# Probability scaling on two engines, half-width projections and a finer gate chain in a diffusion trunk

## The chip, the cores and the metric

The kernel runs on one core of a Trainium2 chip. The metric is the device time of one execution in microseconds (us), median of several runs. A core has five engines that work side by side: TensorE (PE in the profile, its weight loads PEld), VectorE (DVE), ScalarE (ACT), GpSimd (POOL) and SyncE (SP, which here issues DMAs). TensorE writes its results to PSUM, eight banks of 512 f32 columns on 128 partitions.

## The reference, cut to what matters

Two layers of a diffusion trunk over 256 latent and 256 context tokens of width 1024. Each layer is a half-step SwiGLU FFN, a token mixer and another half-step FFN, all with modulated norms. The mixer reads one normalised input `h` and makes three branches from one projection:

```python
qa, ka, va, qb, kb, vb, qm, km, vm, om, gm, gl = split_columns(h @ w_in)
y_a = windowed_attention(rope(qa), ...)                 # branch A, softmax with a sink
y_b = dense_attention(rope(rms_norm(qb)), ...)          # branch B, softmax
y_m = mlstm_mixer((qm, km, vm, om, gm), ...)            # branch C, gates from gm
y = merge(y_a, y_b, y_m, gl, w_branch, w_out)
```

Both attentions have 8 query heads of 64; latent blocks see up to 512 keys, context blocks 256. The mLSTM needs log-sigmoid forget gates, their running sums and a running maximum over each sequence. In the second layer the context tokens have keys and values only, no queries and no output.

## The kernel before, in words

All work is matrix products in split precision. An f32 weight unit of 512 KB (a `raw` tile, 128x1024) is loaded by DMA and turned into a rounded part `hi` by ACT (line 163) and a rest `lo` by DVE (line 164); activations are split likewise (lines 189 and 190). `mm3` (lines 192 to 196) makes one product of three matmuls, hi by hi, hi by lo and lo by hi, summed in PSUM.

The program is a list of tasks, each with the weight units it needs and a function; `run_tasks` issues them in order with loads three units and conversions two units ahead. A scheduler behind it fixes each engine's order of instructions when the program is built, from priorities that follow the program's order; the engines then run in that order and wait on semaphores. Tiles come from pools: eight PSUM banks (`psum`), 13 large SBUF tiles (`slot`), and so on. A new tile of a full pool waits until an old one was last read.

A mixer (`mixer_tasks`, line 830) does the projections `qa`, `qb`, `kk`, `vvg` and `vm` with tasks from `tok_tasks` (line 695): tokens are the stationary operand, 128 at a time, weights the moving one. `qb` and `vm` have 512 columns in four tasks of two k-blocks each (512 KB a task). The first task opens one PSUM bank for each token block (four, or two for `qb` in layer 1), each task adds 6 matmuls of 512 columns to each block, and the last one empties each bank as it finishes: `vm` with a copy on ACT or DVE in turn, `qb` (`q_rows`, line 749) with two ACT reads of the bank, a reduction and, for latent blocks, a rotation on DVE.

Attention (`attn_steps`, line 989) runs in steps, branch A first (x = 0), then branch B (x = 1); 32 steps in layer 0 and 16 in layer 1. A step takes two heads of one block of 128 queries: two score products into two banks, a maximum of each on DVE (line 1016), an exponential of each with its sum on ACT (line 1030), a reciprocal on DVE (line 1039), and the scaling of the two probability tiles E by 1/sum, both on GpSimd (line 1042). Two steps later the tiles are transposed on TensorE (line 1054) into one or two banks and split by ACT and DVE (189, 190), and one step after that multiplied with V (lines 1069 and 1071) into a bank that two steps share.

Other tasks are woven between the steps, to give TensorE work: in branch A the rest of `qb`, `vm`, the mLSTM gates (`mgate_steps`, line 1100) and merge gates computed ahead; in branch B the convolutions. The gates are three tasks: `logsig`, `rows` (16 pairs of small matmuls, then on DVE two copies, five scans and 11 small operations that build the decay rows KR), and `cols`. In layer 0 the first of the four `qb` tasks stands ahead of attention (QC = 1), in layer 1 all of `qb` and the first `vm` task.

Of the kernel before, what the change touches and what calls it, by code (L numbers as in the profile page):

```python
# [10 lines left out]
F32 = mybir.dt.float32  # L11
# [53 lines left out]
class Builder:  # L65
# [41 lines left out]
    def unit_src(self, key):  # L107
# [16 lines left out]
        if kind == "tok":  # L124
            _, l, name, ks, n = key
            src = a["w_" + name][l, ks[0] * P:(ks[-1] + 1) * P, :]
            return src.rearrange("(k p) c -> p k c", p=P), (len(ks), n), True
        if kind == "fm":
# [592 lines left out]

    def by_stream(self, tasks, pre):
# [26 lines left out]
    def q_rows(self, q, src, tb, branch, ss):  # L749
# [9 lines left out]
        sq = self.t512()  # L759
# [3 lines left out]
        if tb < 2:  # L763
            u = self.t512()
            self.rope(u, q, 8, tb, self.cosg[0], self.sing[0], q)
        else:
            self.times_g(q, q, 8, 0)
# [62 lines left out]
    def mixer_tasks(self, l, need_ctx, ms, pre, done, turn):  # L830
# [21 lines left out]
        def qq(x):  # L852
            def f(tb, ps):
                if f"qr{x}" not in R:
                    R[f"qr{x}"] = self.slot([P, 4, T])
                    if x:
                        R["qss"] = self.lp.tile([P, 4, 8], F32, tag="qss", name=self.nm("qss"))
                self.q_rows(R[f"qr{x}"][:, tb, :], ps, tb, x, R["qss"][:, tb, :] if x else None)
            return f
# [25 lines left out]
        def vm(tb, ps):  # L885
# [3 lines left out]
            self.copy(R["vm"][:, tb, :, 0:128], ps.rearrange("p (h d) -> p h d", h=4))  # L889
# [12 lines left out]
        qa = self.tok_tasks(l, "qa", 512, 2, qtb, ms, qq(0))  # L902
        qb = self.tok_tasks(l, "qb", 512, 2, qtb, ms, qq(1))
# [6 lines left out]
        vm_ = self.tok_tasks(l, "vm", 512, 2, range(4), ms, vm)  # L910
# [9 lines left out]
        side = gates[:1] + qb[:1] + gates[1:2] + qb[1:] + vm_[nv:va] + gates[2:] + vm_[va:vb] + qcols(1) + vm_[vb:]  # L920
# [68 lines left out]
    def attn_steps(self, qtb, R):  # L989
# [5 lines left out]
        def score(i):  # L995
# [44 lines left out]
            for e in range(2):  # L1040
                t = E[i][e]
                nc.gpsimd.tensor_scalar(out=t[:, :nkey], in0=t[:, :nkey], scalar1=r[:, e:e + 1], scalar2=None,  # L1042
                                        op0=ALU.mult)
# [56 lines left out]
    def mgate_steps(self, R):  # L1100
# [27 lines left out]
        def rows(_):  # L1128
# [9 lines left out]
            b_r, m_r = RW[:, 2, :], RW[:, 3, :]  # L1138
            i_r, f_r = RW[:, 0, :], RW[:, 1, :]
# [4 lines left out]
            v.tensor_tensor_scan(out=m_r, data0=f_r, data1=i_r, initial=0.0, op0=ALU.add, op1=ALU.max)  # L1144
            KR = self.slot([8, 14, P])
# [33 lines left out]
        return [([], logsig), ([], rows), ([], cols)]  # L1179
# [245 lines left out]
def _layout(inp):  # L1425
# [21 lines left out]
    a["w_qb"] = c(w[:, :, C_QB + qcols])  # L1447
# [47 lines left out]
```

## Time and profile before

| | us |
|---|---|
| median of 3 runs (lowest, highest) | 2273.91 (2273.75, 2274.84) |
| the profiled execution | 2271.84 |
| its span, first to last instruction | 2270.1 |

| engine | busy us | share of the span |
|---|---|---|
| PE | 2195.6 | 97% |
| DVE | 1545.9 | 68% |
| ACT | 984.6 | 43% |
| POOL | 133.0 | 6% |

A row of a timeline gives the start in us from the span's start, the length in us, the engine, the line of the kernel, the instruction, output and inputs by name, shape and how many were merged into the row; in brackets the engine's idle time before it and who ended it. A busy PE counts a matmul until its result has left the array, so matmuls overlap, and the time that one costs is the distance from its start to the next start. Granted clock 1.00 is TensorE's level of 2.4 GHz, 0.50 that of 1.2 GHz.

### The profile page before, as it was taken

How to read it: one execution, taken by the hardware profiler on the slowest of the kernel's cores; microseconds unless marked ns; L12 is line 12 of the kernel's file. 1: busy time of each engine (PE TensorE's matmuls, PEld its weight loads, DVE VectorE, ACT ScalarE, POOL GpSimd, SP SyncE). 2: the span in 40 equal slices, each digit the busy share in tenths (PEclk: the TensorE clock that was granted, in tenths of full speed). 3: DMA queues.
4: the chain of work that ended last, by engine and by line, in shares of the span. 5: the costliest groups of instructions: out<-in, count | busy, mean ns of one | idle time of the engine just before them, and what ended most of it. 6: DMA issues, size and time to landing. Idle time of an engine off the chain costs nothing.

```text
span 2270.1 us, 30607 instructions
## 1 busy us (share of the span) xinstructions
PE 2195.6 (97%) x11666; PEld 1837.6 (81%) x11666; DVE 1545.9 (68%) x2756; ACT 984.6 (43%) x1569; POOL 133.0 (6%) x100
## 2 busy tenths in 40 slices
PE   6999999998999999999999999999999989998998
PEld 4877777787777888888878788777778878997997
DVE  3987775877678664654444378778849787786556
ACT  3322223554588533542222253222226488655444
POOL 0000000013241000000000000000000142000000
PEclk9999999999999999999999999999999999998999
DMA  7665564422213333434433336665634123565554
GB/s 282 214 196 186 165 199 149 125 81 76 94 38 82 119 119 136 142 115 135 129 114 127 103 107 204 195 195 178 223 116 159 57 89 96 167 228 172 189 186 153
DMA packets 126402, 331.36 MB, mean 146 GB/s; under 512 B 12712, under 2 KB 26088, under 8 KB 125488
## 3 DMA queue, kind: packets, MB, share of 16 engines
q1 hardware_dynamic: 111664, 314.02, 43.0%
q10 hardware_dynamic: 14592, 15.40, 2.2%
q8 instruction: 91, 1.49, 0.3%
q14 instruction: 55, 0.45, 0.1%
HBM read 320.91 MB, written 8.47 MB: 145 GB/s over the span
## 4 chain that ended last, share of the span: by engine, by line
PE 84%; DVE 8%; ACT 3%; DMA 2%; issue 2%; POOL 0%; ACTq 0%; POOLq 0%; SPq 0%; DVEq 0%
PE ps L194 26%; PE ps L195 26%; PE ps L196 26%; PE ps L1243 1%; DVE lo L164 1%; DVE sm L1016 1%; ACT t L1030 1%; PE ps L1212 1%; ACT hi L163 1%; PE ps L366 1%; PE ps L1054 1%; PE ps L468 1%; DVE t L190 0%; DVE slot L959 0%; DMA raw<-in_w_gu_dram 0%
## 5 line engine op out<-in xcount | busy, mean ns | idle before, releaser
L163 ACT ACTIVATE hi<-raw 128x1024 fp32r<-128x1024 f32 (+1 forms) x444 | 457.0, 1032 | 766.8 <-PE ps L195 274.7
L194 PE MATMUL ps<-slot,hi 128*128 128x512 f32 (+1 forms) x2232 | 780.5, 351 | 7.7 <-ACT slot L189 5.3
L195 PE MATMUL ps<-slot,hi 128*128 128x512 f32 (+1 forms) x2232 | 776.9, 349 | 0.9 <-DVE slot L190 0.7
L196 PE MATMUL ps<-slot,lo 128*128 128x512 f32 (+1 forms) x2232 | 776.6, 348 | 0.0
L164 DVE TENSOR_TENSOR lo<-raw,hi 128x1024 fp32r<-128x1024 f32 (+1 forms) x444 | 527.1, 1190 | 245.2 <-ACT hi L163 240.7
L194 PEld LDWEIGHTS ps<-slot,hi 128*128 128x128 f32 x2232 | 421.2, 190 | 77.5 <-ACT slot L189 6.6
L195 PEld LDWEIGHTS ps<-slot,hi 128*128 128x128 f32 x2232 | 422.5, 189 | 57.4 <-DVE slot L190 1.7
L196 PEld LDWEIGHTS ps<-slot,lo 128*128 128x128 f32 x2232 | 421.9, 189 | 57.9
L194 PE MATMUL ps<-hi,slot 128*128 128x512 f32 (+2 forms) x1048 | 400.6, 382 | 1.8 <-ACT slot L189 1.1
L196 PE MATMUL ps<-hi,slot 128*128 128x512 f32 (+2 forms) x1048 | 399.5, 382 | 0.0
L195 PE MATMUL ps<-lo,slot 128*128 128x512 f32 (+2 forms) x1048 | 399.5, 381 | 0.0
L358 DVE SCALAR_TENSOR_TENSOR t<-raw,sc,t 128x1024 f32<-128x1024 f32 x224 | 280.5, 1281 | 128.8 <-DMA raw<-in_w_ada_dram 128.5
L1042 POOL TENSOR_SCALAR t<-t,sm 128x512 f32<-128x512 f32 (+1 forms) x96 | 132.9, 1396 | 1767.1 <-DVE sm L1039 1675.7
L194 PEld LDWEIGHTS ps<-hi,slot 128*128 128x128 f32 x1048 | 197.5, 188 | 46.2 <-issue 5.7
L196 PEld LDWEIGHTS ps<-hi,slot 128*128 128x128 f32 x1048 | 197.0, 188 | 39.3
L195 PEld LDWEIGHTS ps<-lo,slot 128*128 128x128 f32 x1048 | 197.3, 188 | 38.8 <-issue 0.2
L189 ACT ACTIVATE slot<-t 128x512 fp32r<-128x512 f32 (+1 forms) x138 | 80.7, 594 | 185.4 <-DVE t L606 160.2
L606 DVE TENSOR_TENSOR t<-ps,t 128x512 f32<-128x512 f32 (+1 forms) x88 | 54.7, 622 | 89.1 <-PE ps L196 87.8
L190 DVE TENSOR_TENSOR slot<-t,slot 128x512 fp32r<-128x512 f32 (+1 forms) x138 | 87.6, 644 | 4.4 <-ACT slot L189 4.1
L1016 DVE TENSOR_REDUCE sm<-ps 128x1 f32<-128x512 f32 (+1 forms) x96 | 54.4, 593 | 22.2 <-PE ps L1015 21.5
L1054 PE MATMUL ps<-ident,t 128*128 128x128 f32 x320 | 47.7, 282 | 18.6 <-POOL t L1042 8.4
L1054 PEld LDWEIGHTS ps<-ident,t 128*128 128x128 f32 x320 | 37.5, 143 | 28.5 <-POOL t L1042 17.3
(198 smaller groups left out, 1670.6 us busy)
## 6 DMA issues: line engine op xcount, KB each, us to landing
raw<-in_w_gu_dram SPq DMA_DIRECT2D x176, 512.0 KB
raw<-in_w_ada_dram SPq DMA_DIRECT2D x128, 512.0 KB
raw<-in_w_down_dram SPq DMA_DIRECT2D x92, 512.0 KB
raw<-in_w_fm_dram SPq DMA_DIRECT2D x64, 512.0 KB
raw<-in_w_br_dram SPq DMA_DIRECT2D x24, 512.0 KB
raw<-in_w_out_dram SPq DMA_DIRECT2D x24, 512.0 KB
slot<-in_w_ada_dram SPq DMA_DIRECT2D x16, 512.0 KB
raw<-in_w_down_dram SPq DMA_DIRECT2D x20, 256.0 KB
```

What stands on the lines that cost most here:

```text
L163: self.nc.scalar.activation(out=hi, in_=raw, func=AF.Copy)
L164: self.nc.vector.tensor_tensor(out=lo, in0=raw, in1=hi.bitcast(F32), op=ALU.subtract)
L189: self.nc.scalar.activation(out=hi, in_=src, func=AF.Copy)
L190: self.nc.vector.tensor_tensor(out=lo, in0=src, in1=hi.bitcast(F32), op=ALU.subtract)
L194: mm(out, lh, rh, start=start, stop=False, **kw)
L195: mm(out, lh, rl, start=False, stop=False, **kw)
L196: mm(out, ll, rh, start=False, stop=stop, **kw)
L358: v.scalar_tensor_tensor(out=acc, in0=units[0], scalar=c, in1=acc, op0=ALU.mult, op1=ALU.add)
L606: nc.vector.tensor_tensor(out=hid[:, :W], in0=ps[:, :W], in1=hid[:, :W], op=ALU.mult)
L1016: v.tensor_reduce(out=mx[:, e:e + 1], in_=ps[:, :nkey], axis=AX.X, op=ALU.max)
L1042: nc.gpsimd.tensor_scalar(out=t[:, :nkey], in0=t[:, :nkey], scalar1=r[:, e:e + 1], scalar2=None, op0=ALU.mult)
L1054: nc.tensor.transpose(pt[:, n * P:(n + 1) * P], e[n % 2][:, kb * P:(kb + 1) * P], self.ident)
```

## The change

Three things are changed.

1. In the attention step GpSimd scales only the first of the two tiles. The second goes to ACT in branch A and to DVE in branch B.
2. `qb` and `vm` are taken in two halves of 256 columns, each half in two tasks of four k-blocks (still 512 KB a task, now contiguous). Two token blocks share one PSUM bank, so that a half holds two banks (one for `qb` in layer 1) where the whole held four (two). A block's half is emptied as it finishes in the second task. The evacuations `q_rows` (branch B) and `vm` work on 256 columns, twice as often.
3. The gate task `rows` becomes three tasks: `rows` (matmuls and copies), `scans` and `decays`. In layer 0 the first four gate tasks are woven with the three `qb` tasks that are left.

```diff
+        if kind == "half":
+            _, l, name, h, g = key
+            return a["w_" + name][l, h, g], (4, 256), True
...
+    def half_tasks(self, l, name, tbs, ms, evac):
+        ds = {}
+        def mk(h, g):
+            def fn(units):
+                u = units[0]
+                for tb in tbs:
+                    if g == 0 and tb % 2 == 0:
+                        ds[h, tb // 2] = self.psum().rearrange("p (b c) -> p b c", b=2)
+                    ps = ds[h, tb // 2][:, tb % 2, :]
+                    for x in range(4):
+                        lh, ll = ms["hi"][g][:, x, tb * P:(tb + 1) * P], ms["lo"][g][:, x, tb * P:(tb + 1) * P]
+                        self.mm3(ps, lh, ll, u[0][:, x, :], u[1][:, x, :], g == x == tb % 2 == 0, g == 1 and x == 3,
+                                 skip_group_check=True)
+                    if g:
+                        evac(tb, h, ps)
+            return ([("half", l, name, h, g)], fn)
+        return [mk(h, g) for h in range(2) for g in range(2)]
...
-        sq = self.t512()
+        sq = self.t512()[:, :256]
...
-            u = self.t512()
-            self.rope(u, q, 8, tb, self.cosg[0], self.sing[0], q)
+            u = self.t512()[:, :256]
+            self.rope(u, q, 4, tb, self.cosg[0], self.sing[0], q)
         else:
-            self.times_g(q, q, 8, 0)
+            self.times_g(q, q, 4, 0)
...
-            self.copy(R["vm"][:, tb, :, 0:128], ps.rearrange("p (h d) -> p h d", h=4))
+            self.copy(R["vm"][:, tb, 2 * h:2 * h + 2, 0:128], ps.rearrange("p (h d) -> p h d", h=2))
...
-        qb = self.tok_tasks(l, "qb", 512, 2, qtb, ms, qq(1))
+        qb = self.half_tasks(l, "qb", qtb, ms, qqb)
...
-        vm_ = self.tok_tasks(l, "vm", 512, 2, range(4), ms, vm)
+        vm_ = self.half_tasks(l, "vm", range(4), ms, vm)
...
-        side = gates[:1] + qb[:1] + gates[1:2] + qb[1:] + vm_[nv:va] + gates[2:] + vm_[va:vb] + qcols(1) + vm_[vb:]
+        side = weave(gates[:4], qb) + vm_[nv:va] + gates[4:] + vm_[va:vb] + qcols(1) + vm_[vb:]
...
             for e in range(2):
-                t = E[i][e]
-                nc.gpsimd.tensor_scalar(out=t[:, :nkey], in0=t[:, :nkey], scalar1=r[:, e:e + 1], scalar2=None,
-                                        op0=ALU.mult)
+                t = E[i][e][:, :nkey]
+                if e and x == 0:
+                    nc.scalar.activation(out=t, in_=t, func=AF.Copy, scale=r[:, e:e + 1])
+                else:
+                    (v if e else nc.gpsimd).tensor_scalar(out=t, in0=t, scalar1=r[:, e:e + 1], scalar2=None, op0=ALU.mult)
...
-        return [([], logsig), ([], rows), ([], cols)]
+        return [([], logsig), ([], rows), ([], scans), ([], decays), ([], cols)]
```

The weights of `qb` and `vm` are laid out by halves on the host, outside the measured time.

## Rows read from the trace of the kernel before

**Rows 1.** The page's head: the span of the profiled execution.
```profile
span 2270.1 us, 30607 instructions
```

**Rows 2.** Busy time by stretch: attention A and B of layer 0, between, layer 1.
```profile
480.00:604.00 124.00, 118.11 (x641) 96.76 (x640) 90.69 (x240) 64.33 (x145) 38.98 (x30) 1.00 0.21 70
604.00:705.00 101.00, 90.58 (x499) 75.81 (x498) 72.17 (x152) 75.86 (x139) 42.81 (x35) 0.98 0.27 79
705.00:1780.00 1075.00, 1072.04 (x5135) 880.90 (x5134) 695.32 (x1169) 400.36 (x591) 0.00 (x0) 1.00 0.44 141
1780.00:1848.00 68.00, 61.06 (x391) 51.29 (x389) 54.83 (x137) 37.32 (x82) 25.32 (x16) 0.97 0.18 60
1848.00:1903.00 55.00, 48.36 (x314) 42.39 (x313) 42.90 (x88) 46.22 (x78) 25.74 (x16) 0.97 0.22 73
```
Columns: stretch, its length, busy us (instructions) of PE, PEld, DVE, ACT and POOL, granted clock, DMA share, GB/s.

**Rows 3.** PE's waits, 480 to 604 us: total us, times, longest.
```profile
PE ps L1054 <- DVE t L190: 3.2, 1, 3.2
PE ps L1069 <- ACT t L1030: 2.0, 1, 2.0
```

**Rows 4.** PE's waits, 604 to 705 us.
```profile
PE ps L1054 <- POOL t L1042: 6.0, 8, 1.2
```

**Rows 5.** PE's waits, 1780 to 1848 us.
```profile
PE ps L1069 <- DVE t L190: 2.2, 2, 1.7
```

**Rows 6.** PE's waits, 1848 to 1903 us.
```profile
PE ps L1054 <- POOL t L1042: 2.4, 3, 1.2
```

**Rows 7.** Groups of instructions by shape on POOL: busy us, mean ns, idle before.
```profile
L1042 POOL TENSOR_SCALAR t<-t,sm 128x512 f32<-128x512 f32 x64 | 102.7, 1616 | 1698.9 <-DVE sm L1039 1648.0 <-ACT t L189 18.1 <-ACT sm L1036 13.3
```

**Rows 8.** Timeline at 647 to 651 us: one step's scalings, then its transposes.
```profile
647.61 3.10 POOL L1042 TENSOR_SCALAR t<-t,sm 128x512 f32<-128x512 f32 x2 [3.75 <-DVE sm L1039]
...
650.77 0.98 PE L1054 MATMUL ps<-ident,t 128*128 128x128 f32 x7 [1.21 <-POOL t L1042]
```

**Rows 9.** Timeline of DVE: start of `rows`' chain, and the split behind it.
```profile
511.83 0.67 DVE L1137 COPY slot<-ps 8x512 f32<-8x512 f32 x1
...
520.22 0.67 DVE L190 TENSOR_TENSOR t<-ps,t 128x512 fp32r<-128x512 f32 x1
```

**Rows 10.** Timeline of PE: matmuls of 512 columns, then of 256.
```profile
522.22 0.40 PE L195 MATMUL ps<-slot,hi 128*128 128x512 f32 x1
...
527.30 0.40 PE L196 MATMUL ps<-slot,lo 128*128 128x512 f32 x1
...
455.06 0.28 PE L195 MATMUL ps<-lo,slot 128*128 128x256 f32 x1
...
458.90 0.28 PE L195 MATMUL ps<-lo,slot 128*128 128x256 f32 x1
```

**Rows 11.** Groups by shape on DVE and ACT, for prices.
```profile
L356 DVE TENSOR_SCALAR t<-raw,sc 128x1024 f32<-128x1024 f32 x32 | 23.5, 750 | 14.5 <-DMA raw<-in_w_ada_dram 14.3 <-DMA t<-in_norm_g_dram 0.2
...
L164 DVE TENSOR_TENSOR lo<-raw,hi 128x1024 fp32r<-128x1024 f32 x416 | 507.8, 1223 | 227.6 <-ACT hi L163 223.1 <-PE ps L196 1.4
...
L164 DVE TENSOR_TENSOR lo<-raw,hi 128x512 fp32r<-128x512 f32 x20 | 13.8, 689 | 16.4 <-ACT hi L163 16.4
...
L453 ACT ACTIVATE t<-slot,sm 128x1024 f32<-128x1024 f32 x10 | 11.5, 1145 | 11.4 <-DVE sm L220 11.4
```

**Rows 12.** Timeline of DVE and POOL where both work at once.
```profile
1872.36 0.62 DVE L1024 TENSOR_TENSOR sm<-sm,qsc 128x2 f32<-128x2 f32 x1
...
1870.74 3.10 POOL L1042 TENSOR_SCALAR t<-t,sm 128x512 f32<-128x512 f32 x2 [5.76 <-DVE sm L1039]
...
1896.17 1.21 DVE L164 TENSOR_TENSOR lo<-raw,hi 128x1024 fp32r<-128x1024 f32 x1
...
1896.35 4.00 POOL L1042 TENSOR_SCALAR t<-t,sm 128x512 f32<-128x512 f32 x2 [5.80 <-DVE sm L1039]
```

**Rows 13.** Groups by shape on ACT: prenorm's second reader of a bank.
```profile
L478 ACT ACTIVATE t<-ps,modT,Amod 128x256 f32<-128x256 f32 x54 | 27.8, 562 | 30.0 <-DVE t L476 22.0 <-PE ps L468 8.0
```

**Rows 14.** Busy time by stretch: one at the lower clock.
```profile
622.10:625.40 3.30, 3.30 (x14) 2.92 (x12) 1.48 (x4) 2.82 (x7) 0.00 (x0) 0.50 0.00 1
```

More of the change, by code (lines that the diff above doesn't have):

```diff
@@ L850, in vv, with qqa, qqb @@
             self.copy(R["gm"][:, tb, :], ps[:, 256:272])
[L852 to L859, printed above, removed]
+        def qqa(tb, ps):
+            if "qr0" not in R:
+                R["qr0"] = self.slot([P, 4, T])
+            self.q_rows(R["qr0"][:, tb, :], ps, tb, 0, None)
+        def qqb(tb, h, ps):
+            if "qr1" not in R:
+                R["qr1"] = self.slot([P, 4, T])
+                R["qss"] = self.lp.tile([P, 4, 8], F32, tag="qss", name=self.nm("qss"))
+            self.q_rows(R["qr1"][:, tb, 256 * h:256 * h + 256], ps, tb, 1, R["qss"][:, tb, 4 * h:4 * h + 4])
         def qcols(x):
@@ L883, in unspill, with vm @@
                 nc.sync.dma_start(self.X[s], self.spill[s])
-        def vm(tb, ps):
+        def vm(tb, h, ps):
             if "vm" not in R:
@@ L901, in mixer_tasks @@
         vt = self.tok_tasks(l, "vvg", 272, 2, range(4), ms, vv)
-        qa = self.tok_tasks(l, "qa", 512, 2, qtb, ms, qq(0))
-        qb = self.tok_tasks(l, "qb", 512, 2, qtb, ms, qq(1))
+        qa = self.tok_tasks(l, "qa", 512, 2, qtb, ms, qqa)
+        qb = self.half_tasks(l, "qb", qtb, ms, qqb)
         conv = [self.conv_task(l, c, ms, R, need_ctx) for c in range(8)]
@@ L1137, in rows, with scans @@
                 v.tensor_copy(RW[:, q, :], ps[:8, :])
-            b_r, m_r = RW[:, 2, :], RW[:, 3, :]
-            i_r, f_r = RW[:, 0, :], RW[:, 1, :]
+            R["RW"] = RW
+        def scans(_):
+            RW = R["RW"]
+            i_r, f_r, b_r, m_r = (RW[:, q, :] for q in range(4))
             for b in range(4):
@@ L1144, in rows, with decays @@
             v.tensor_tensor_scan(out=m_r, data0=f_r, data1=i_r, initial=0.0, op0=ALU.add, op1=ALU.max)
+        def decays(_):
+            RW = R.pop("RW")
+            i_r, f_r, b_r, m_r = (RW[:, q, :] for q in range(4))
             KR = self.slot([8, 14, P])
@@ L1446, in _layout @@
     a["w_qa"] = c(w[:, :, C_QA + qcols])
-    a["w_qb"] = c(w[:, :, C_QB + qcols])
+    halves = lambda m: c(m.reshape(2, 2, 4, P, 2, 256).transpose(0, 4, 1, 3, 2, 5))
+    a["w_qb"] = halves(w[:, :, C_QB + qcols])
     a["w_kk"] = c(np.concatenate([w[:, :, C_KA:C_KA + 128], w[:, :, C_KB:C_KB + 128]], axis=2))
@@ L1450, in _layout @@
     a["w_vvg"] = c(np.concatenate([w[:, :, C_VA:C_VA + 128], w[:, :, C_VB:C_VB + 128], w[:, :, C_GM + gcols]], axis=2))
-    a["w_vm"] = c(w[:, :, C_VM:C_VM + 512])
+    a["w_vm"] = halves(w[:, :, C_VM:C_VM + 512])
     a["w_om"] = c(w[:, :, C_OM:C_OM + 512])
```

## The prediction

> **What bounds the kernel now.** I read busy time by stretch first, then PE's waits in the stretches that fall short. Outside the mixers' attention TensorE is the bound: between the two attentions it is busy 1072.04 of 1075 us [rows 2], so nothing done to other engines there can show. The four attention stretches are where the change acts. PE is idle there for 124.0 - 118.1 = 5.9 us in branch A and 101.0 - 90.6 = 10.4 us in branch B of layer 0, and for 6.9 and 6.6 us in layer 1 [rows 2]. That is 29.8 us, and it is nearly all that the change can win. On top stand short stretches at the lower clock: in one of 3.3 us the granted clock is 0.50 [rows 14], and the means of 0.98, 0.97 and 0.97 in three of the stretches [rows 2] say there is about one in each.
>
> Who ends the idle time differs by branch. In layer 0, branch A, two waits make 5.2 of the 5.9 us: one of 3.2 us for a bank that the split on DVE frees late, one of 2.0 us for a bank that an exponential frees late [rows 3]. In branch B, GpSimd's scaling ends 6.0 of the 10.4 us, in 8 waits [rows 4]. In layer 1, branch A waits mostly for splits on DVE (2.2 us in the largest group, [rows 5]), and branch B for GpSimd (2.4 us, [rows 6]) and for DVE. DVE is busy 90.7 of 124, 72.2 of 101, 54.8 of 68 and 42.9 of 55 us, ACT 75.9 of 101 and 46.2 of 55 us in the two B stretches [rows 2]. So PE is ahead, but DVE and ACT have no more than a fifth to a quarter to spare, and every step is a chain through all of them.
>
> **Scaling on two engines.** Today the two tiles of a step are scaled one after the other, 1.6 us each [rows 7], so the second is ready 3.1 us after the reciprocal. The timeline shows which of the two hurts: after the pair of 3.10 us one transpose has gone ahead and the other seven wait 1.21 us for the second [rows 8]. With the second tile on DVE or ACT the pair is ready when GpSimd's one is, 1.6 us earlier or a little less. In branch B I count half of the 6.0 + 2.4 us as won: the waits for the second tile go, those for the first stay. That is -4.2 us; the ends are 0 (something else comes last) and -8.4.
>
> The work does not vanish. A two-input operation costs 1223 ns at 1024 columns and 689 at 512 [rows 11], so 2 x 689 - 1223 = 155 ns are fixed. The one-input scaling on DVE takes 750 ns at 1024 [rows 11]; with the same fixed part it is 0.45 us at 512 columns and 0.30 at 256. Branch B gives DVE 8 x 0.45 + 8 x 0.30 = 6.0 us in layer 0 and 8 x 0.45 = 3.6 us in layer 1. The trace has no 512-column scaling from SBUF; the ends are half of 750 ns and all of it. DVE rises from 71 to 77% of layer 0's B stretch and from 78 to 85% of layer 1's. Maxima and splits queue behind it, and PE waits for those already. I charge a quarter of the 9.6 us, +2.4 us; the ends are 0 and all of it. ACT's scaled copy is 1145 ns at 1024 [rows 11], by the same split 0.65 us at 512 and 0.40 at 256: 8.4 us in layer 0's A stretch, where ACT is busy 64.3 of 124 us, and 5.2 us in layer 1's, 37.3 of 68 [rows 2]. Exponentials, splits and conversions queue behind it. With half of ACT free I charge nothing; without that cover it would be a quarter of 13.6 us, +3.4.
>
> GpSimd and DVE meet more often now. The trace has both orders. A DVE operation with two SBUF inputs that is already running holds GpSimd up: behind the 1.21 us conversion at 1896.17 the pair that starts at 1896.35 takes 4.00 us where 3.10 is usual. In the other order a tiny DVE operation, 0.08 us behind the start of the pair's second scaling (1870.74 + 1.54), takes 0.62 us for two columns [rows 12]: it ends 0.7 us into GpSimd's 1.56 us, so it waits for the first part of that instruction, not for all of it. DVE's scaling comes right behind the reciprocal on its own engine, while GpSimd has to be told by a semaphore, so I expect DVE first and GpSimd up to 0.45 us later. That is why half of the waits stay in the sum above.
>
> The Trainium skill, "SBUF — State Buffer", section "Who interferes with whom", says that whoever of DVE in a two-port mode and GpSimd issues first holds the shared pair for the whole instruction and the other fully blocks. The first order agrees, the second only in part (0.62 us of 1.56). Taken at its word in the bad order, it is the third rival.
>
> **Halves and shared banks.** `qb` and `vm` have 14 products of one token block (4 + 4 in layer 0, 2 + 4 in layer 1), each 24 matmuls of 512 columns: 336, which become 672 of 256. From 522.22 to 527.30 lie 22 matmuls of 512, 231 ns each; from 455.06 to 458.90 lie 33 of 256, 116 ns each [rows 10]. Two halves cost 1 to 2 ns more than the whole: 336 x 2 = +0.7 us, with PE the bound there. The doubled weight loads stay hidden, as they are in these rows. Loads and conversions keep their number and size. Evacuations double in count, at 155 ns fixed each: a few us on DVE and ACT over both layers, hidden where PE is busy; I charge nothing.
>
> What it gives is room. Through most of branch A four of eight banks are held by an open `qb` or `vm`; two score banks, one for transposes and one for output are all that is left to attention, and the two large waits of [rows 3] are waits for banks. With two held, both should go or shrink. For the first there is a second reason: the chain of `rows` keeps DVE from 511.83 on, and the split that PE waits for stands behind it at 520.22, 8.4 us later [rows 9]. Cut in three, it lets attention's maxima and splits in between; that moves 8 us of DVE work, it removes none, and the last gate task comes one or two side tasks later, with its reader far behind. I take -4.0 of the 5.2 us in layer 0 (ends 0 and -5.2). In layer 1 all of `qb` is before attention, only `vm` holds banks, and the waits are for DVE, which keeps its work: I take -2.0 (ends +2, as five gate tasks now fill steps that have no other product, and -4).
>
> What it costs is a new wait. The second block of a bank may write only when the first has been read out. The trace shows that a bank is passed on as a whole: prenorm reads two separate halves of one bank on DVE and then on ACT, and ACT sat idle 22.0 us before its half until DVE was done, in 7 waits [rows 13], though no data go between them. There are 14 blocks, so 7 such bank pairs per half and 14 handovers. PE can do the other bank's block meanwhile, 12 x 116 ns = 1.4 us, or attention, which stands in the same queue. A reader that is not delayed needs less than that. I charge 0.1 us each, +1.5 us; the ends are 0 and the first rival.
>
> **Sum.** -4.2 + 2.4 + 0.7 - 4.0 - 2.0 + 1.5 = -5.6 us. Of three stretches at the lower clock, each standing behind long waits, I let one go: 3.4 us at half speed is 1.7 us of work, taken as -1.2. Together -6.8 us, against the profiled execution of 2271.84 (span 2270.1, [rows 1], and 1.7 around it): 2265.0. The median of the runs is 2.1 us above that execution, so I forecast **2267 us**.
>
> **Rivals.** *No change,* **2273**. Every step runs through DVE, ACT and PE, and the order on each is fixed beforehand. A wait of 1 us for GpSimd that goes shows the next one, for a maximum or a split, right behind; won and lost waits balance, and only the 0.7 us of columns and the odd wait remain. For it: in branch B no engine is idle more than 30%, and besides GpSimd four other producers end PE's waits. Against: the 3.2 and 2.0 us waits of [rows 3] have a clear cause that the change removes. Chance 0.27. That the change doesn't do what it says is the same case: a scaling ordered so late on DVE that the pair is ready no earlier.
>
> *The bank handover, slower.* If the reader of the first block stands behind a conversion (1.22 us, [rows 11]) before its reads (0.56 us each for 256 columns, [rows 13], two for `qb`, one for `vm`), PE is held 1.22 + 1.12 - 1.4 = 0.9 us at a `qb` handover and about 0.4 at a `vm` one even with the other bank's block as cover, and 2.3 and 1.8 without. With 6 and 8 handovers, all uncovered: 14 + 14 = 28 us; with half of them, 14 us, against the sum without its 1.5, -8.3: 2273.9 + 14 - 8.3 = **2280**. It decides from where readers begin over 1 us after the block's last matmul. The Trainium skill speaks for the wait itself: "PSUM — Partial Sum Buffer", section "PSUM bank collisions raise a hardware error", wants PSUM guarded by bank, not by address; the 22.0 us of [rows 13] agree. Chance 0.10.
>
> *The shared port, slower.* If GpSimd comes first and DVE's scaling waits for its whole 1.56 us (0.8 at 256 columns, by halving), branch B adds 8 x 2.0 + 8 x 1.1 = 25 us of DVE time in layer 0, where 28.8 are free, and 16 us in layer 1, where 12.1 are [rows 2]: layer 1 overruns by 4 us, and a third of layer 0's 25 shows, 8 us; with the -6 of branch A, 2273.9 + 12 - 6 = **2280**. It decides from where DVE has other work between the reciprocal and the scaling. Chance 0.08.
>
> **How the numbers follow.** Forecast 0.55, no change 0.27, the slower two 0.18. About 0.2%, 4.5 us, is what a measurement of this kernel can tell from no change: faster means below 2269.4, slower above 2278.5. The far ends of the gains (-5.2, -4, -8.4 and three clock stretches of 1.7) give 2251; I put the low end at 2255, since all at once is unlikely, and the high end just over the slower rivals, 2281, leaving some 0.05 below and 0.13 above. The forecast's own range is 2255 to 2269.
>
> **What would show it.** Right: the wait of 3.2 us for a split near 521 and that of 2.0 us for an exponential are gone; PE's waits for GpSimd in branch B fall from 8.4 to about 4 us; PE's idle time falls from 29.8 to about 23; DVE's new scaling takes 0.45 us and starts ahead of GpSimd's. Wrong: PE's waits before the second block of `qb` or `vm` for ACT's or DVE's evacuation (handover); scalings of 1 us and more on DVE (port); waits for maxima and splits that grow by what those for GpSimd lose (no change).

## The result, and the profile after

The changed kernel is slower: a median of 2286.39 us (2284.68 to 2291.26) against 2273.83 us (2273.63 to 2274.84) for the kernel before on the same chip, a ratio of 1.0060 (95% interval 1.0048 to 1.0072). That is 12.6 us, and outside the predicted range. The profiled execution took 2286.34 us, its span is 2284.6 us: 14.5 us more than before's.

Busy time by stretch in the changed kernel, with the same columns as [rows 2] and bounds at the same work (attention A and B of layer 0, between, attention A and B of layer 1):

```profile
480.00:609.00 129.00, 116.91 (x782) 103.75 (x781) 92.88 (x260) 74.92 (x171) 19.16 (x15) 0.97 0.22 71
609.00:715.00 106.00, 92.47 (x522) 77.56 (x522) 76.65 (x165) 74.86 (x139) 21.63 (x17) 0.98 0.24 70
715.00:1791.00 1076.00, 1073.65 (x5201) 883.96 (x5200) 698.46 (x1186) 401.54 (x595) 0.00 (x0) 1.00 0.44 142
1791.00:1859.00 68.00, 61.52 (x454) 55.75 (x453) 53.38 (x132) 41.72 (x91) 12.51 (x8) 0.95 0.17 56
1859.00:1916.00 57.00, 50.58 (x333) 45.01 (x332) 46.07 (x95) 46.73 (x80) 12.81 (x8) 0.97 0.27 80
```

PE is idle for 12.1, 13.5, 6.5 and 6.4 us in the four attention stretches, 38.5 us where [rows 2] gave 29.8. GpSimd's load is halved, as the change says (19.2 + 21.6 us in layer 0 against 39.0 + 42.8), and PE has more to wait for. Its waits from 480 to 609 us (total us, times, longest):

```profile
PE ps L1164 <- DVE s L1154: 5.7, 1, 5.7
PE ps L1164 <- DVE s L1153: 3.0, 1, 3.0
PE ps L197 <- DVE slot L810: 1.8, 1, 1.8
PE ps L1039 <- DVE slot L810: 1.5, 1, 1.5
```

The waits of 3.2 and 2.0 us in [rows 3] are gone, as predicted. In their place stand 8.7 us at L1164, the small matmuls of the gate task `rows`. From 609 to 715 us, branch B, the waits are now these:

```profile
PE ps L1083 <- POOL t L1072: 4.3, 4, 1.5
PE ps L1083 <- DVE t L193: 2.6, 2, 2.0
PE ps L1098 <- DVE t L193: 2.1, 2, 1.3
PE ps L197 <- DVE slot L986: 1.5, 1, 1.5
```

GpSimd's 6.0 us of [rows 4] fell to 4.3, and DVE's splits (L193) hold PE for 4.7 us. PE's timeline shows how the first hole looks:

```profile
487.51 0.28 PE L199 MATMUL ps<-hi,slot 128*128 128x256 f32 x1
490.76 0.38 PE L1164 MATMUL ps<-ident,s 128*8 128x128 f32 x2 [2.97 <-DVE s L1153]
...
492.29 0.38 PE L1165 MATMUL ps<-anti,s 128*8 128x128 f32 x2
498.36 0.58 PE L1164 MATMUL ps<-ident,s 128*8 128x128 f32 x2 [5.69 <-DVE s L1154]
...
503.42 1.04 PE L1083 MATMUL ps<-ident,t 128*128 128x128 f32 x8
```

The last product of `qb` starts at 487.51. Then `rows` stands on PE and waits twice for the log-sigmoid's short operations on DVE. The granted clock is 0.50 from 495.7, inside the second hole, to 502.5, so that the second half of `rows` takes 3.2 us from its first start to its last where the first took 1.6. The first transposes start at 503.42, 7.3 us later than before (496.13). Nothing of `qb` or `vm` fills the holes, though most of both is still to be done; why, the experiments show.

A table by stretch, from PE's timelines, makes the runs comparable. A layer's attention is taken from its first score product to its last product with V; the figures are differences to the kernel before in us (whose own are 221.5, 1079.9 and 123.9). The medians stand against the kernel before timed beside each run on the same chip.

The stretches come from one profiled execution of each kernel, and that lay up to 5.3 us below the median of its runs (halves, one read) and up to 3.0 above it (gates cut, with scaling); before's lay 2.1 below. What lies ahead of layer 0's attention and behind layer 1's is hardly touched by any part, and still lies -2.6 to +3.2 us from before's; differences that are smaller say little by themselves. The bounds also don't always hold the same work. With the halves alone layer 0's attention has weight products worth 535 of 512 columns where before has 527, 1.9 us more at 231 ns each. And where `vm` is in halves in shared banks, PE waits 4.4 us directly ahead of layer 1's first score, where before it waits 0.7, and this counts in the column "between"; before, then the halves alone:

```profile
1784.73 0.47 PE L1012 MATMUL ps<-slot,slot 128*128 128x512 f32 x1 [0.71 <-DVE slot L826]
```

```profile
1793.06 0.77 PE L1039 MATMUL ps<-slot,slot 128*128 128x512 f32 x1 [4.39 <-DVE slot L810]
```

For those kernels the last two columns are read together.

| kernel | median, to its before | ratio, 95% | attention layer 0 | between | attention layer 1 |
|---|---|---|---|---|---|
| changed | +12.6 | 1.0048 to 1.0072 | +13.5 | +2.1 | -1.5 |
| scaling alone | +5.0 | 1.0015 to 1.0034 | +4.1 | -1.6 | +2.3 |
| halves alone | +4.5 | 1.0011 to 1.0029 | +7.7 | +2.5 | -3.1 |
| gates alone | -5.8 | 0.9960 to 0.9983 | +0.9 | +1.1 | -6.4 |
| gates cut, old place | -8.1 | 0.9953 to 0.9978 | -1.4 | 0.0 | -6.3 |
| halves and gates | +11.4 | 1.0036 to 1.0064 | +11.8 | +3.3 | -0.2 |
| changed, `rows` behind `qb` | +9.0 | 1.0020 to 1.0045 | +10.8 | +0.8 | -2.2 |
| changed, one read | +8.0 | 1.0023 to 1.0048 | +9.0 | +1.8 | -3.2 |
| halves, own banks | +4.6 | 1.0007 to 1.0024 | -0.1 | +2.5 | +2.1 |
| halves, one read | +5.4 | 1.0009 to 1.0027 | +5.1 | +2.3 | -3.1 |
| changed, own banks | +18.5 | 1.0067 to 1.0094 | +11.7 | +2.1 | +2.6 |
| ACT scaling, branch A | +0.5 | 0.9993 to 1.0010 | +2.8 | -0.1 | +0.6 |
| DVE scaling, branch B | +3.1 | 1.0005 to 1.0023 | +4.3 | -1.7 | +2.3 |
| gates cut, with scaling | -4.2 | 0.9974 to 0.9992 | +3.8 | -1.5 | -0.9 |
| changed, `vm` whole | +3.3 | 1.0008 to 1.0025 | +12.9 | -0.6 | -2.6 |
| changed, three causes undone (last run) | -5.4 | 0.9964 to 0.9985 | +2.9 | -1.1 | -2.2 |

### The profile page after: what moved, and what is told of

Same layout as the page of the kernel before. It is cut to its first block, busy times and chain, and to the rows that moved or that the text cites. A ratio compares the mean times of both kernels' runs of the same rounds, so it can differ in the third digit from the quotient of the medians.

```text
span 2284.6 us, 31294 instructions
## 1 busy us (share of the span) xinstructions
PE 2200.6 (96%) x12002; PEld 1857.6 (81%) x12002; DVE 1557.0 (68%) x2808; ACT 1000.8 (44%) x1609; POOL 66.3 (3%) x52
## 4 chain that ended last, share of the span: by engine, by line
PE 84%; DVE 8%; ACT 4%; DMA 3%; issue 1%; POOL 0%; ACTq 0%; SPq 0%; DVEq 0%; POOLq 0%
PE ps L197 26%; PE ps L198 26%; PE ps L199 26%; DVE lo L167 1%; PE ps L1279 1%; DVE sm L1043 1%; ACT t L1057 1%; PE ps L1248 1%; ACT hi L166 1%; PE ps L369 1%; PE ps L1083 1%; DVE slot L986 1%; PE ps L471 1%; DMA raw<-in_w_gu_dram 0%; DMA raw<-pre 0%
## 5 line engine op out<-in xcount | busy, mean ns | idle before, releaser
L197 PE MATMUL ps<-hi,slot 128*128 128x512 f32 (+2 forms) x1160 | 420.8, 363 | 4.0 <-DVE slot L810 1.8
L198 PE MATMUL ps<-lo,slot 128*128 128x512 f32 (+2 forms) x1160 | 417.1, 360 | 0.0
L199 PE MATMUL ps<-hi,slot 128*128 128x512 f32 (+2 forms) x1160 | 417.0, 360 | 0.0
L197 PEld LDWEIGHTS ps<-hi,slot 128*128 128x128 f32 x1160 | 218.2, 188 | 46.3 <-issue 6.1
L199 PEld LDWEIGHTS ps<-hi,slot 128*128 128x128 f32 x1160 | 217.8, 188 | 35.9 <-DVE slot L193 0.2
L198 PEld LDWEIGHTS ps<-lo,slot 128*128 128x128 f32 x1160 | 218.5, 188 | 34.7
L1072 POOL TENSOR_SCALAR t<-t,sm 128x512 f32<-128x512 f32 (+1 forms) x48 | 66.1, 1377 | 1844.8 <-DVE sm L1066 1771.4
L193 DVE TENSOR_TENSOR slot<-t,slot 128x512 fp32r<-128x512 f32 (+1 forms) x138 | 87.4, 642 | 6.1 <-ACT slot L192 5.8
L606 ACT ACTIVATE t<-ps 128x512 f32<-128x512 f32 (+1 forms) x88 | 46.4, 528 | 22.2 <-DVE t L429 16.5
```

The lines of the kernel that those rows point to most:

```text
L193: self.nc.vector.tensor_tensor(out=lo, in0=src, in1=hi.bitcast(F32), op=ALU.subtract)
L197: mm(out, lh, rh, start=start, stop=False, **kw)
L198: mm(out, lh, rl, start=False, stop=False, **kw)
L199: mm(out, ll, rh, start=False, stop=stop, **kw)
L1072: (v if e else nc.gpsimd).tensor_scalar(out=t, in0=t, scalar1=r[:, e:e + 1], scalar2=None, op0=ALU.mult)
```

## The experiments

### One part at a time

My first theory was the place of `rows` alone: in layer 0 the change lets it follow `logsig` directly, where a `qb` task stood between them. The change with `rows` put back tests it, and each part of the change by itself tests what else could be behind it.

```diff
-        side = weave(gates[:4], qb) + vm_[nv:va] + gates[4:] + ...
+        side = gates[:1] + qb[:1] + gates[1:2] + qb[1:2] + gates[2:3] + qb[2:] + gates[3:4] + vm_[nv:va] + gates[4:] + ...
```

> The changed kernel with one thing moved: in layer 0 the gate task rows stands behind the first qb task again (logsig, qb, rows, qb, scans, qb, decays), as it did before; everything else is as changed. Theory G (the place of rows): in the changed kernel the 32 small matmuls of rows stand on PE ahead of the qb products and wait 5.7 + 3.0 us for logsig's chain on DVE, and the clock falls to 0.50 behind them for 6.8 us; the first transposes came 7.3 us later than before. With a qb task in between, both waits go and about 7 to 8 us come back: 2278 to 2280 us, with the 5 us or so that arise later in the trace still there. Rival H (halves and shared banks cost it): rows is not the cause, the wait moves to the next bank, 2284 to 2287. Rival S (scaling on two engines costs it): also 2284 to 2287.

Measured: 2282.08 us, +9.0, between the two ranges. Layer 0's attention got back 2.7 us of its 13.5, not 7 to 8. The wait at L1164 is gone, and one of 5.5 us for GpSimd's scaling stands at the first transposes instead. The place of `rows` is not the whole cause; the hole was there without it.

The three parts, each added alone to the kernel before (part 1: the scaling lines of the diff; part 2: `half_tasks` and what it needs; part 3: the cut gates and the `side` line):

> The kernel before with part 1 alone: the second probability tile is scaled on ACT in branch A and on DVE in branch B; projections and gates as before. My forecast's terms for this part give -4.2 + 2.4 = -1.8: 2272 us. Theory G: it costs nothing, 2270 to 2274. Rival S (more work on DVE and ACT, or the port that DVE shares with GpSimd, outweighs the earlier tile): layer 0's branch B lost 3.3 us in the changed kernel and layer 1 about 3; if the scaling is behind both, 2277 to 2281.

Measured: 2278.07 us, +5.0. Neither the -1.8 of my terms nor nothing: rival S holds for this part.

> The kernel before with part 2 alone: qb and vm in halves of 256 columns, two token blocks in a bank; scaling and gates as before (rows behind the first qb task). My forecast's terms give +0.7 for the columns, -4 and -2 for the banks won, +1.5 for the handovers: -3.8, 2270 us. Theory G: it costs nothing or wins a little, 2269 to 2275. Rival H (the wait for the handover of a shared bank, or evacuations twice as many): 2278 or more.

Measured: 2277.58 us, +4.5, with +7.7 us in layer 0's attention and -3.1 in layer 1's. That is far from the -3.8 of my terms and 0.4 us under rival H's range, so something in the halves costs; what, the trace below shows. The -3.1 is no gain by itself: the wait of 4.4 us ahead of layer 1's first score stands in "between", +2.5, and together they are -0.6.

> The kernel before with part 3 alone: the gate task rows cut in three and the first four gate tasks woven with the three qb tasks, so that rows comes right behind logsig; scaling and halves as before. Theory G: the matmuls of rows wait for logsig's chain on PE, 2279 to 2282 us; less, 2274 to 2278, if the scheduler puts qb's matmuls of 512 columns between those of rows. Rivals H and S: the gates cost nothing, 2270 to 2275.

Measured: 2267.32 us, -5.8, below every range. Theory G fell here: with `qb` in whole width the same order of tasks is a gain, since the scheduler lays matmuls of `qb` between those of `rows` and PE waits 0.9 us there.

The trace of the halves alone shows the cause of its hole, first PE, then ACT (L785 is `qb`'s copy out of the bank, L786 its Square):

```profile
485.49 0.28 PE L199 MATMUL ps<-hi,slot 128*128 128x256 f32 x1
...
486.90 0.28 PE L199 MATMUL ps<-hi,slot 128*128 128x256 f32 x1
...
493.99 0.69 PE L1081 MATMUL ps<-ident,t 128*128 128x128 f32 x2 [5.45 <-POOL t L1069]
495.54 1.54 PE L1081 MATMUL ps<-ident,t 128*128 128x128 f32 x6 [0.86 <-POOL t L1069]
...
498.16 0.41 PE L197 MATMUL ps<-hi,slot 128*128 128x256 f32 x1
```

```profile
486.05 0.38 ACT L785 ACTIVATE slot<-ps 128x256 f32<-128x256 f32 x1
487.22 0.38 ACT L785 ACTIVATE slot<-ps 128x256 f32<-128x256 f32 x1 [0.78 <-PE ps L199]
...
495.33 0.38 ACT L786 ACTIVATE t<-ps 128x256 f32<-128x256 f32 x1
```

In the second task of the first half PE does blocks 0 and 2 (their last matmuls start at 485.49 and 486.90) and stops. Blocks 1 and 3 write the other halves of the same two banks. ACT copies block 0 out at 486.05, but reads the bank again, for the Square, only at 495.33, behind two steps' exponentials and 9.8 us after the start of the block's last matmul. So between the first scores and the first transposes PE has 24 matmuls of 256 columns, 2.8 us, where the kernel before had 39 of 512, 9.1 us. The scheduler, which knows of the reads, has put block 1 (498.16) behind the transposes. That is why the page never shows PE waiting for ACT here: it waits for whatever comes next in the fixed order, GpSimd's scaling in this kernel, `logsig` in the changed one. There the Square comes at 514.62, and block 1 follows at 515.05:

```profile
492.48 0.65 ACT L785 ACTIVATE slot<-ps 128x256 f32<-128x256 f32 x2
...
504.05 1.09 ACT L192 ACTIVATE t<-ps 128x512 fp32r<-128x512 f32 x2 [5.39 <-PE ps L1083]
...
514.62 0.38 ACT L786 ACTIVATE t<-ps 128x256 f32<-128x256 f32 x1
```

ACT's load is not what holds the Square: ACT stood idle for 5.39 us before 504.05, waiting for the transposes, with the Square still to come in its order. Why the scheduler puts it there was not tested. One reason may be that the Square writes a new tile of the pool `t512`, which has eight, of which every step in flight holds two; no run tried more.

### The handover, tested

If the handover is the cause, it goes with banks of their own, and with one read instead of two.

```diff
-                    if g == 0 and tb % 2 == 0:
-                        ds[h, tb // 2] = self.psum().rearrange("p (b c) -> p b c", b=2)
-                    ps = ds[h, tb // 2][:, tb % 2, :]
+                    if g == 0:
+                        ds[h, tb] = self.psum()[:, :256]
+                    ps = ds[h, tb]
```

> Part 2 alone as in the run with the halves alone, but every token block of a half opens a bank of its own (four for a half, two for qb in layer 1) instead of sharing one. Theory H (handover): with the halves alone PE has only 24 matmuls of 256 columns between the first scores and the first transposes, because blocks 1 and 3 of qb may write only when ACT has read blocks 0 and 2 twice, and the second read (Square, 495.33 us) stands behind two steps' exponentials, 8.4 us after the block's last matmul; PE idles 5.5 us there and the clock falls for 10.2 us. Without sharing, the 5.5 us wait goes: 2271 to 2274 us. Rival C (the width of 256 columns, the doubled evacuations or the order of the tasks cost it): no change to the halves alone, 2276 to 2280.

Measured: 2278.1 us, 1.0007 to 1.0024, no change in the whole. By stretch it is what the theory said and something it didn't: layer 0's attention fell from +7.7 to -0.1 us. The wait of 5.5 us only shrank to 3.0, but the time at the lower clock, which had begun inside that wait, fell from 13.7 to 3.4 us. Layer 1's attention rose from -3.1 to +2.1, as four open banks are what the halves were to save; that this is the reason is argued, not shown. As a test of the total the expectation failed; as one of the place it held.

```diff
-        nc.scalar.activation(out=sq, in_=src, func=AF.Square)
+        nc.scalar.activation(out=sq, in_=q, func=AF.Square)
```

> Part 2 alone, banks shared, but qb's Square reads the copy in SBUF instead of the bank, so that a bank is free after ACT's first read (486.05 us with the halves alone, 0.3 us after the block's last matmul is complete). Theory H: the second reader is what holds blocks 1 and 3, so the 5.5 us wait for GpSimd's scaling goes and the time is as with banks of their own, 2271 to 2274 us. Rival C: no change to the halves alone, 2276 to 2280. If only the number of banks matters (with banks of their own faster, here not), it is not the reader.

Measured: 2278.95 us, 1.0009 to 1.0027; the profiled execution, 2273.61 us, lay below the median of its runs. In that trace layer 0's attention is at +5.1 instead of +7.7, and 48 matmuls of `qb` stand between scores and transposes. The wait for the scaling is 3.3 us, and one of 2.3 us for ACT's copy (L785) is new: the handover under its own name, with one reader left. By the total the expectation failed, and as a test of the reader this run is inconclusive. Both totals lie in rival C's range, so for the halves alone the handover rests on the stretches; the runs within the whole change have to decide.

The two tests were repeated within the whole change, together with parts 2 and 3 without the scaling:

> Parts 2 and 3 together, scaling on GpSimd as before. If the parts add up, the halves (+4.5) and the gates (-5.8) give 2272 us. Theory H+G: they don't, since rows ahead of qb needs qb's products behind it to hide its wait, and the shared banks take just these away: 2279 to 2283 us, with the waits of 5.7 and 3.0 us for logsig on PE in layer 0 as in the changed kernel.

Measured: 2284.32 us, +11.4, 1 us above the expected range, and the same waits at `rows`, 6.1 + 3.0 us. The parts don't add up: +4.5 and -5.8 make +11.4. The halves take away the products that hid `rows`, and `rows` moved ahead then holds PE longer than GpSimd's scaling did: +11.8 us in layer 0 against +7.7 of the halves alone.

> The whole change, with one thing altered: qb's Square reads the copy in SBUF, so that a shared bank is handed on after ACT's first read. Theory H+G (the handover leaves PE without qb work in layer 0's branch A, and rows, moved ahead, then waits for logsig on PE): the matmuls of blocks 1 and 3 stand before the first transposes again, 24 of them between the two halves of rows; the waits of 5.7 and 3.0 us shrink to under 4 together, 2279 to 2283 us (changed: 2286). If the place of rows alone is the cause: 2285 to 2288, the waits stay.

Measured: 2280.97 us, +8.0, 4.6 less than the change. The time is the expected one. PE's timeline:

```profile
492.45 0.64 PE L1165 MATMUL ps<-anti,s 128*8 128x128 f32 x2
493.02 0.58 PE L197 MATMUL ps<-hi,slot 128*128 128x256 f32 x1
...
496.55 0.28 PE L199 MATMUL ps<-hi,slot 128*128 128x256 f32 x1
498.91 0.38 PE L1164 MATMUL ps<-ident,s 128*8 128x128 f32 x2 [2.08 <-DVE s L1154]
```

Blocks 1 and 3 stand between the two halves of `rows` and fill 3.6 us of the hole; the second wait is 2.1 us instead of 5.7, and the low clock lasts 3.4 us instead of 6.8. The first stays at 3.0, so that together they are 5.1 us and not under 4: nothing that stands ahead of it became free. One source operand of one instruction did this.

> The whole change, but every token block of a half has a bank of its own. Theory H+G: the waits of rows in layer 0 shrink as with one read; layer 1 pays for the banks, as the halves alone did with banks of their own (4 to 5 us there): 2279 to 2284 us. Place of rows alone: 2285 to 2288.

Measured: 2291.42 us, +18.5: wrong, the slowest of all. Layer 1 pays as expected (+2.6 against the change's -1.5); it is layer 0 that got back too little, 11.7 against 13.5. `rows` still waits 6.3 us. PE does all four blocks ahead of `rows`, but the next half needs four banks, and those of the first are held until its Squares, which begin at 515.96. So it isn't sharing as such that matters. In the kernel before, the four tasks of `qb` add into the same four banks, and 22 us of products need no bank and no reader to go on. Cut in halves, only 11 us do; behind them every product needs a reader on ACT or DVE to have finished. Whether it waits for a shared bank or for a new one is secondary. That is argued from the counts and this run; no run varies the width alone.

### What the gates gave

> The kernel before with the gate task cut in three, but in layer 0 rows kept behind the first qb task that is left (logsig, qb, rows, qb, scans, qb, decays); layer 1's order is that of the run with the gates alone. Theory: the gates' gain of 5.8 us was layer 1's (that trace ran level with before up to 1750 us and was 5 us ahead at 1930), where the chain of rows lets maxima and splits in between: again 2266 to 2269 us. Rival: it was the weaving with qb in layer 0, 2271 to 2274.

Measured: 2264.83 us, -8.1, a little more than expected; it is faster than both kernels and the fastest of this study. Layer 1's attention is at -6.3 us, as with the gates alone; layer 0's at -1.4 against +0.9. Of these 2.3 us, PE's idle time makes 0.4; the rest goes with one stretch more at the lower clock (6.8 us against 3.4), and the intervals of the two medians overlap. So with `qb` whole the place of `rows` is worth little. DVE before, then with the gates cut, where `scans` ends and the rest of the chain begins:

```profile
1801.96 1.19 DVE L1144 TENSOR_TENSOR_SCAN slot<-slot 8x512 f32<-8x512 f32 x1
1803.07 0.25 DVE L1151 TENSOR_TENSOR slot<-slot 8x128 f32<-8x128 f32 x1
...
1806.25 0.67 DVE L190 TENSOR_TENSOR t<-ps,t 128x512 fp32r<-128x512 f32 x1
```

```profile
1800.93 1.19 DVE L1147 TENSOR_TENSOR_SCAN slot<-slot 8x512 f32<-8x512 f32 x1
1802.04 0.65 DVE L1016 TENSOR_REDUCE sm<-ps 128x1 f32<-128x512 f32 x1
1802.62 0.67 DVE L190 TENSOR_TENSOR t<-ps,t 128x512 fp32r<-128x512 f32 x1
```

The split that PE needs starts 1.7 us behind the start of the last scan instead of 4.3. No DVE work was removed, as predicted (1545.8 us in all, against 1545.9); the rest of the chain was put off. PE's idle time in layer 1's attention fell from 12.9 to 8.8 us, and the time at the lower clock from 6.8 to 3.4.

### What the scaling cost

```diff
+                if e and x == 0:
+                    nc.scalar.activation(out=t, in_=t, func=AF.Copy, scale=r[:, e:e + 1])
```

> The kernel before with the second tile scaled on ACT in branch A alone; branch B on GpSimd twice, as before. Both branches together cost 5.0 us, where my terms gave -1.8. In that trace layer 0's branch A ended 1.4 us later and layer 1's not later. Theory D (DVE in branch B makes most of the cost): 2273 to 2275 us. Theory A (ACT's queue makes it: exponentials and splits behind the scaled copy): 2276 to 2278.

Measured: 2274.06 us, a ratio of 1.0001 (0.9993 to 1.0010): nothing, as theory D said. Layer 0's +2.8 in the table is not ACT's: PE is idle there for 16.0 us, against 16.3 before, and this execution spent 10.2 us at the lower clock, against 3.4.

```diff
+                eng = v if e and x else nc.gpsimd
+                eng.tensor_scalar(out=t, in0=t, scalar1=r[:, e:e + 1], scalar2=None, op0=ALU.mult)
```

> The kernel before with the second tile scaled on DVE in branch B alone; branch A on GpSimd twice, as before. With both branches, layer 0's B stretch ended about 1 us later and layer 1's 2.8 us later. Theory D (DVE's splits come later behind the scalings, and what PE waited for on GpSimd it now waits for on DVE): 2275 to 2278 us. Theory A: the gain of the forecast, 2270 to 2273.

Measured: 2276.65 us, +3.1 (1.0005 to 1.0023). Theory D holds. PE's waits from 604 to 708 us in this kernel:

```profile
PE ps L1054 <- POOL t L1043: 3.9, 4, 1.5
PE ps L1054 <- DVE t L190: 2.6, 2, 2.0
PE ps L1069 <- DVE t L190: 2.1, 2, 1.3
PE ps L194 <- DVE slot L959: 1.5, 1, 1.5
```

GpSimd's waits fell by 2.1 us from the 6.0 of [rows 4]. Those for DVE's splits at these two lines rose to 4.7 from a single one of 1.0, and one of 1.5 for a convolution on DVE is new: an exchange with a loss.

> The fastest kernel so far (gates cut, rows behind qb, 2264.8 us) with the scaling on two engines added and nothing else. Theory D (DVE's scalings put off its splits and cost as much as they win for GpSimd's waits): the +5.0 of the scaling alone comes again, 2268 to 2271. Rival: with rows' chain cut DVE is freer, and the scaling wins what was forecast, 2260 to 2264.

Measured: 2269.44 us, -4.2 against its before, where the gates cut alone had -8.1: 4.0 more (the two ran on different chips, so the differences are compared). Theory D again: with the gate chain cut the scaling costs about the same.

### Layer 1, and all causes together

```diff
-        vm_ = self.half_tasks(l, "vm", range(4), ms, vm)
+        vm_ = self.tok_tasks(l, "vm", 512, 2, range(4), ms, vm)
```

> The whole change, but vm in whole width as before (512 columns, four tasks into four banks of their own); only qb is in halves. Layer 1 is where the halves of vm lie under attention: with the gates alone it ended 6 us earlier than before, in the changed kernel 3 us later; PE waits 4.4 us there for the first scores, with 24 of vm's products held because ACT reads blocks 0 and 2 only 16 us after their last matmul. Theory H (vm's handover eats the gates' gain): the 4.4 us wait goes and 5 to 9 us come back, all behind 1760 us: 2277 to 2281. Rival: it is the scaling that eats it, 2284 to 2287, layer 1 unchanged.

Measured: 2276.94 us, +3.3, 9.3 less than the change, at the lower edge of theory H. The wait of 4.4 us for layer 1's first scores is gone. In the changed kernel `vm`'s blocks 0 and 2 had their last matmul at 1794.41, and ACT copied them out here:

```profile
1827.70 0.38 ACT L204 ACTIVATE slot<-ps 128x256 f32<-128x256 f32 x1
...
1828.23 0.39 ACT L204 ACTIVATE slot<-ps 128x256 f32<-128x256 f32 x1 [0.15 <-ACT slot L204]
```

That is 33 us later (the 16 us of the expectation are those of the halves alone). Until then the other two blocks could not fill anything; the first of their matmuls waits for the copy:

```profile
1828.13 0.39 PE L197 MATMUL ps<-hi,slot 128*128 128x256 f32 x1 [0.31 <-ACT slot L204]
```

By the stretches only 4.4 of the 9.3 us lie there and in attention; the rest lies outside, where profiled executions differ anyway, so the size is less sure than the sign.

The last run undoes the three causes and keeps the scaling, the cut gates and `qb`'s halves:

> The whole change with all its handovers and the place of rows undone: vm whole, qb in halves with Square reading the SBUF copy, rows behind the first qb task; the scaling stays on two engines and the gate task stays cut in three. Theory: what is left is the cut gates (-8.2 alone), the scaling (+5.0 alone) and qb's halves without their handover (0 to +3): 2268 to 2274 us. Rival (the parts cost each other by something else): 2276 or more.

Measured: 2268.24 us, -5.4 (0.9964 to 0.9985), as the theory said. 18.0 us lie between this kernel and the changed one, and they differ in nothing but the width of `vm`, the source of one Square and the place of `rows`. Undone one at a time these gave 9.3, 4.6 and 3.6 us, 17.5 in all: here the parts add up. Against the gates cut with scaling (-4.2), which this kernel differs from only by `qb` in halves with one read of the bank, it is no dearer, so the width of 256 columns and the doubled evacuations of `qb`, rival C, cost nothing that shows.

## Why the prediction was wrong

**The bound** was read rightly: between the attentions PE is busy 1073.65 of 1076 us, and everything happened in attention.

**The sum.** The forecast added its terms to -6.8 us, and the change measured +12.6. Alone, scaling, halves and gates are +5.0, +4.5 and -5.8, so +3.7 together; 8.9 us arise only where they meet. Halves and gates make +11.4 where their own sum is -1.3. No term and no rival of the prediction was for that.

**The step that failed** is the cost under "Halves and shared banks": "PE can do the other bank's block meanwhile [...] A reader that is not delayed needs less than that. I charge 0.1 us each, +1.5 us." I had taken the price from the first reader. The bank is free after the last one, and that stood 9.8 us (Square, halves alone), 28.5 us (Square, changed) and 33 us (`vm`'s copy, changed) behind the block's last matmul, because the evacuation has a low place in ACT's fixed order. The term was +1.5; the halves alone are at +7.7 in layer 0's attention, of which 1.9 is work that lay elsewhere before, and with banks of their own at -0.1. The first rival named this mechanism and its condition, "readers begin over 1 us after the block's last matmul", and its 2280 is nearer to the result than the forecast. That is partly luck: it counted 0.4 to 2.3 us for a handover behind a conversion, not readers that come 9.8 to 33 us late. Its sign in the profile was wrong too: I looked for PE's waits for the evacuation, and in the changed kernel there is one of 0.3 us, since the order set when the program is built had already moved the blocks behind. The trace shows such a cost as products that are missing ahead of another wait. That a bank is passed on as a whole, which I took from [rows 13], these runs bear out: in the changed kernel ACT's copy of one block of `vm` ends at 1828.08, and the first matmul on the other block's columns, which had waited for it, starts at 1828.13. The Trainium skill, "PSUM — Partial Sum Buffer", section "PSUM bank collisions raise a hardware error", wants PSUM guarded by bank and not by address; that wait agrees.

**The second error** is in the same part: "it removes none, and the last gate task comes one or two side tasks later, with its reader far behind." I followed the last gate task back to its reader and not the first ones forward to PE. `rows` puts 32 matmuls on PE, and with the change they come right behind the operations that they need. With `qb` whole that shows little in layer 0 (+0.9 against -1.4, most of it the clock); without `qb`'s products to hide it, it costs 4 us (+11.8 against +7.7), 3.5 of them PE's idle time (22.5 against 19.0 us).

**The cut of the chain** was mis-sized the other way. I gave it part of -4.0 in layer 0 and a loss of up to 2 in layer 1 ("five gate tasks now fill steps that have no other product"). It brought -6.3 in layer 1, most of the gain of the fastest kernel.

**Banks.** The two waits of [rows 3] went, but what they gave was paid for elsewhere. In layer 1, where I had -2.0, the halves alone are at -3.1 behind the first score and +2.5 ahead of it, -0.6 in all: the gain that I forecast does not show. Halves and gates together are at -0.2 and +3.3 there, where the gates alone have -6.4 and +1.1. Why the gates' gain goes was not settled.

**Scaling.** "PE's waits for GpSimd in branch B fall from 8.4 to about 4 us": 6.0 + 2.4 became 4.3 + 0. The gain's term was right. The charge of "a quarter of the 9.6 us" for DVE was not: the scalings took 13.2 us of DVE (groups below), and PE's waits for splits and convolutions alone grew by 5.2 us in layer 0's branch B. The "no change" rival described it, with a loss in place of a balance: +3.1 us. (Its "no engine is idle more than 30%" leaves out GpSimd, busy for 42.81 of 101 us in [rows 2].)

```profile
L1072 DVE TENSOR_SCALAR t<-t,sm 128x512 f32<-128x512 f32 x16 | 10.0, 624 | 0.2
L1072 DVE TENSOR_SCALAR t<-t,sm 128x256 f32<-128x256 f32 x8 | 3.2, 402 | 0.1
```

**ACT at nothing** held: 1.0001 (0.9993 to 1.0010) with ACT's scaling alone.

**The clock.** I let one of three stretches at the lower level go. In the changed kernel there are five in attention, 20.5 us together against 10.2, and each begins inside a wait of PE or at most 1.3 us behind one. PE was busy for 17.6 us of them, against 9.8 before; by an estimate these 7.8 us more at half speed cost 3.9 us, about as much as the largest terms of my sum. With the 8.7 us of added idle time that makes 12.6 of the 14.5 us by which the span grew. Not every wait has such a stretch: with 16.6 us of idle time in layer 0's attention the last run has none there, and ACT's scaling alone, with 16.0, has three.

**The port.** The third rival did not come: no wide DVE scaling took more than 0.81 us.

## What to carry to other kernels

Open accumulators are not only a cost in banks: products that add into them need no reader, and here that made them the filler that hid other waits. Before a bank is shared or emptied earlier, find its last reader in that engine's order, not its first, and ask what fills PE until then. When a task is cut or moved, follow what each piece puts on every engine to the next instruction there; and where a wait was hidden by other work, test the parts together, since two changes that are harmless or good alone can take each other's cover away.

## What the runs showed of the hardware

DVE and GpSimd scaled side by side, and the order was not the one I had expected: GpSimd starts first in 15 of the changed kernel's 16 wide pairs, in 11 of them by 0.31 to 0.35 us. Three of them, DVE's lines and then GpSimd's:

```profile
643.48 0.63 DVE L1072 TENSOR_SCALAR t<-t,sm 128x512 f32<-128x512 f32 x1
647.34 0.49 DVE L1072 TENSOR_SCALAR t<-t,sm 128x512 f32<-128x512 f32 x1
...
667.60 0.81 DVE L1072 TENSOR_SCALAR t<-t,sm 128x512 f32<-128x512 f32 x1
```

```profile
643.14 1.56 POOL L1072 TENSOR_SCALAR t<-t,sm 128x512 f32<-128x512 f32 x1 [5.01 <-DVE sm L1066]
647.40 1.86 POOL L1072 TENSOR_SCALAR t<-t,sm 128x512 f32<-128x512 f32 x1 [2.69 <-DVE sm L1066]
...
667.44 1.57 POOL L1072 TENSOR_SCALAR t<-t,sm 128x512 f32<-128x512 f32 x1 [3.60 <-DVE sm L1066]
```

In two pairs the two start within 0.06 us of each other; DVE's then takes 0.49 us, near the estimate of 0.45, and GpSimd's 1.85 and 1.86 instead of 1.56. In 13 pairs GpSimd is ahead by 0.15 to 1.07 us; DVE's takes 0.61 to 0.81 us and GpSimd's 1.56 or 1.57. In the last, with GpSimd 0.60 us ahead, neither is longer (0.48 and 1.57). So one of the two mostly pays, up to 0.33 us, and in most pairs DVE's operation begins and ends inside GpSimd's.

The Trainium skill, "SBUF — State Buffer", section "Who interferes with whom", says of DVE in a two-port mode and GpSimd that whoever issues first holds the shared pair for its whole instruction while the other fully blocks. That one of them pays agrees; that DVE is shut out until GpSimd's 1.56 us are over does not. Which mode DVE's scaling runs in, no row here shows.
